# The fourth quarter of the summed shares: turned by the DMA engines in place of TensorE

## The chip, the core and the metric

The kernel runs on one core of one Trainium2 chip. The time is the device time of one launch in microseconds. Its engines here are TensorE (matmuls, PE in the profile, its weight loads PEld), VectorE (DVE), ScalarE (ACT), GpSimd (POOL) and SyncE (SP), which only issues DMAs. Each engine works through its own queue in order. Tiles lie in SBUF, and matmuls write to PSUM.

## The reference

Two layers over 512 tokens of 1024 channels, each made of a SwiGLU, a mixer (attention and a short convolution) and a second SwiGLU:

```python
def swiglu(h, w_gate, w_up, w_down):
    return (jax.nn.silu(h @ w_gate) * (h @ w_up)) @ w_down

for l in range(DEPTH):
    x = x + 0.5 * swiglu(rms_norm(x, ffn1_norm[l]), ffn1_wg[l], ffn1_wu[l], ffn1_wd[l])
    h = rms_norm(x, mix_norm[l])
    z = h @ w_in[l]
    ...
    x = x + jnp.concatenate([attn_out, conv_out], axis=-1) @ w_out[l]
    x = x + 0.5 * swiglu(rms_norm(x, ffn2_norm[l]), ffn2_wg[l], ffn2_wu[l], ffn2_wd[l])
return rms_norm(x, final_norm)
```

The inner width is 2816. All is float32.

## The kernel before, in words

The residual `x` lies transposed in SBUF for the whole run: 1024 channels are eight chunks of 128 (`xs[0]` to `xs[7]`), channels on the partitions and 512 tokens along a row. Two neighbouring chunks share a tile, so there are four pair tiles `xpair`, which the trace prints with the name `x`.

A float32 matrix is multiplied in three products. Each operand is split into a high part (`wh`, `xh`, `ah`: a ScalarE copy, L228 or L470) and a low part (`wl`, `xl`, `al`: a VectorE subtraction), and high by high, high by low and low by high are summed in PSUM (L318, L319, L321). Weights come from HBM as units of 512 KB into tiles `raw`, of which there are eight; SP issues their loads (L210) and `need_split` makes the high and low parts, two groups ahead of the matmuls. There are three `wh` and three `wl`.

A SwiGLU is a list of stages. An inner one (three of the four; the last one of the kernel ends in another way) runs `INNER`: blocks "p" and "w" of gate and up products, two stages "s" and a closing stage ("d", (9, 10)). A stage "s" multiplies by a part of `w_down` with seven products in place of eight. Its products have the tokens on the partitions, so their sum cannot be added to `x` as it is. The class `Apart` keeps this sum as tiles `apart`, one for each of four token tiles and two halves of the channels. It is treated in four quarters (o, t): half o of the channels and half t of the tokens. Quarter (0, 1) is the last to be complete, with the last product of the second stage "s".

A quarter comes back to `x` in one of two ways:

- by DMA: `Apart.send` lays the 16-bit halves of each float32 apart (ScalarE, L141, two copies of 128x1024 16-bit words) and SP issues two transposing DMAs (L909) into a tile `turned`. `Apart.back` joins the halves again (ScalarE, L922, two copies) and adds the result to `x` (VectorE, L926, two additions of 128x512).
- by TensorE: if a quarter was not sent, `Apart.back` makes eight 128x128 transposes with the identity into PSUM (L932) and adds from there (VectorE, L937, two additions).

Before the change, quarters (0, 0), (1, 1) and (1, 0) are sent at steps 3, 4 and 5 of the second stage "s" (`SENT_AT`), and (0, 1) is turned by TensorE.

The closing stage runs `down` over chunks in the order 4, 5, 6, 7, 0, 1, 2, 3. Each chunk takes 12 matmuls into an accumulator; VectorE adds half of it to the chunk of `x` (L1266). `BACK_AT` says behind which chunk a quarter is added back. Then `after(k)` prepares chunk k for the next stage's norm (class `into`): `norm.take` makes the gained high part on ScalarE (L470) and the low part on VectorE (L471), `norm.square` makes the squares on ScalarE (L476, L479, tile `nsq`) and sums them on VectorE (L480, tile `nacc`). `FINAL_AT` lets chunks 4 and 5 wait until behind chunk 5.

The next stage starts with groups of 24 matmuls over all eight chunks, again in the order 4 to 7, 0 to 3 for the first group. The sum of squares is split as well (`sqh` on ScalarE, `sql` on VectorE, L228), and two matmuls with ones (L535, tile `ssq`) stand behind the second chunk of the second group.

The loads of the weights of the next stage are held back (`state["hold"]`) through the last stage "s" and freed in the closing stage at chunk 5. `state["behind"]` then puts them in SP's queue behind the instruction `apart.last`, the last transposing DMA that was issued; at chunk 0 that is lifted.

ScalarE's and VectorE's queues are not written out by hand at this place: a scheduler orders the instructions when the program is built, within what the code ties down with `issue_after`.

Of the kernel before, what the change touches and what calls it, by code (L numbers as in the profile page):

```python
# [49 lines left out]


SENT_AT = {3: (0, 0), 4: (1, 1), 5: (1, 0)}
BACK_AT = {4: ((0, 1),), 5: ((1, 0),)}
FINAL_AT = {4: (), 5: (4, 5)}
STREAM_BACK_AT = {9: 0, 11: 1, 16: 2, 18: 3}
SCORES_AT = (5, 6, 7, 8, 9, 10, 12, 13)
# [19 lines left out]
def trunk_kernel(  # L76
# [35 lines left out]
    def g2(name, dt=F32, shape=(P, S)):  # L112
        return work.tile(list(shape), dt, tag="g2", bufs=14, name=name)
# [63 lines left out]
    def turn_rows(i):  # L177
        n = rows[i].shape[0]
        rp = psum("aux", [P, n], f"par_ps{i}")
        nc.tensor.transpose(rp, rows[i], ident[:n, :n])  # L180
        nc.scalar.copy(par[:, 16 * i : 16 * i + n], rp)
# [163 lines left out]
    def halves_of(n, wide, last):  # L345

        blocks = list(range(0, n, wide))
        return blocks[len(blocks) // 2 :] + blocks[: len(blocks) // 2] if last else blocks

    def down(rhs, fresh=False, last=False):  # L350

        wide = abreast(len(rhs))
        for c in halves_of(KC, wide, last):
            n, hi, lo = take_split()
            if fresh and c == 0:
                yield from enumerate(level(n, hi, lo, rhs, wide))
                continue
            for j in range(wide):
                cols = slice(j * P, (j + 1) * P)
                own = (f"{n}_{j}", hi[:, :, cols], lo[:, :, cols])  # L360
                tag = ("sc", "sc", "aux", "aux")[j] if fresh else "mm"
                yield c + j, group(rhs, own=own, tag=tag)
# [576 lines left out]
    def ahead(ops, at):  # L939
        return lambda step: ops.make(*at.get(step, ()))  # L940


    def ffn(norm, stages, after=None, late=None):
# [3 lines left out]
        def plain(b):  # L947
            gates = []

            def gate(acc):  # L950
                t = g2(f"gate_{norm.i}_{b}_{len(gates)}")
                nc.vector.tensor_mul(t, acc, norm.inv)
                nc.scalar.activation(t, t, AF.Silu)
                nc.vector.tensor_mul(t, t, norm.inv)
                gates.append(t)

            hi, lo = parts_of(f"a_{norm.i}_{b}")

            def up(j, acc):
                t = gates[j]  # L960
                nc.vector.tensor_mul(t, acc, t)
                split(hi[:, j, :], lo[:, j, :], t)

            if norm.i:
                accs = norm.groups(4)
                gate(accs[0])
                gate(accs[1])
                norm.scale()
                up(0, accs[2])
                norm.make("b11")  # L970
                up(1, accs[3])
            else:
                gate(opening[0])
                gate(opening[1])
                accs = norm.groups(4, opening)
                up(0, accs[2])
                up(1, accs[3])
                norm.scale((0,))
                norm.make("b11")
                norm.scale((1,))  # L980
            acts[b] = (hi, lo)
# [171 lines left out]
        def shared(b):  # L1153
            return Seven(lambda: [raws[b], raws[b + 2]], room_form, f"s_{norm.i}_{b}")

        def joined(between):


            def step(n):
                if n == 3:  # L1160
                    crossing[0].join_half(0)
                if n == 4:
                    crossing.pop(0).join_half(1)
                if crossing and isinstance(crossing[-1], Tail):
                    crossing[-1].during(n)
                between(n)

            return step
# [17 lines left out]
        def flush(n=1, *tag):  # L1186
            for _ in range(n):
                if pending:
                    pending.pop(0)(*tag)
# [3 lines left out]
        apart = Apart(f"{norm.i}")  # L1193
        for i, (what, b) in enumerate(stages):
            if what == "w" and stages[i + 1][0] == "s":
                ops = shared(sevens[0])
                winograd2(b, ahead(ops, {3: ("b11",), 4: ("b21",), 5: ("t2",), 6: ("t3",)}))
            elif what == "w":
                if after is None and b == 1:
                    end = apart = Finale()  # L1200
                between = late if b == 5 else end.step if end else None
                winograd2(b, between)
            if what == "s" and end:
                ends = [
                    Seven(full, None, f"e_{n}")
                    for n, full in enumerate((lambda b=b: [raws[b + 4], raws[b + 6]], raws[b + 8]))
                ]

                def between(step):
                    if 0 < step < 3:  # L1210
                        flush(2, "mm")
                    for at, n, operand in ((3, 0, "b11"), (4, 1, "b11"), (5, 0, "t2"), (6, 1, "t2")):
                        if step == at:
                            ends[n].make(operand)

                share(ops, 0.5, joined(between), apart, still=kept)
            elif what == "e":
                end.last(ends, kept)
                return
            elif what == "s" and b == sevens[0]:  # L1220
                then = shared(sevens[1])
                share(
                    ops,
                    0.5,
                    joined(ahead(then, {3: ("b11",), 4: ("b21",), 5: ("t2",), 6: ("t3",)})),
                    apart,
                    still=kept,
                )
            elif what == "s":

                def between(step):
                    if step == 1:
                        crossing[0].rejoin(1)
                    if step in (4, 5):
                        with tc.issue_after(state["rest"]):
                            crossing[0].parts(step - 4)
                    if step in SENT_AT:
                        apart.send(*SENT_AT[step])
                    if step == 0:
                        state["hold"] = closing[norm.i // 3 * 2 + norm.i % 3 // 2]  # L1240
                    if step == 6:
                        apart.back(0, 0)
                        apart.back(1, 1)

                share(then, 0.5, between, apart, behind=(1, 2, 3), on=kept)
            if what == "p":
                plain(b)
                if late:
                    turn_rows(1)
            if what != "d":  # L1250
                continue
            rhs = [(acts[k][0][:, j, :], acts[k][1][:, j, :]) for k in b if k in acts for j in range(2)]
            final = i + 1 == len(stages)
            if final:
                after.norm.order = halves_of(KC, 1, True)
            for c, acc in down(rhs, b == (0,), final):
                if b == (0,):
                    made = {0: "b21", 2: "t2", 5: "t3"}
                    if c in made:
                        norm.make(made[c])  # L1260
                if b == (0,) and norm.i == 0:
                    part = g2(f"down_{c}")
                    nc.scalar.activation(part, acc, AF.Copy, scale=0.5)
                    nc.gpsimd.dma_start(out=xs[c], in_=part, accum_op=ALU.add)
                else:
                    nc.vector.scalar_tensor_tensor(  # L1266
                        xs[c], acc, 0.5, xs[c], op0=ALU.mult, op1=ALU.add
                    )
                flush()
                if final:  # L1270
                    if c == 5:
                        state["hold"], state["behind"] = None, apart.last
                    if c == 0:
                        state["behind"] = None
                    for quarter in BACK_AT.get(c, ()):
                        apart.back(*quarter)
                    for k in FINAL_AT.get(c, (c,)):
                        after(k)

# [459 lines left out]
    for l in range(DEPTH):  # L1739
        n1, n2, n3 = Norm(3 * l + 1), Norm(3 * l + 2), Norm(3 * l + 3)  # L1740
        ffn(norm, INNER, into(n1), None if l else bias_steps())
        mix(l, n1, into(n2))
        if l + 1 < DEPTH:
            ffn(n2, INNER, into(n3))
        else:
            ffn(n2, LAST)
        norm = n3
# [30 lines left out]
```

## Time and profile before

| | |
|---|---|
| median of 3 runs | 1627.56 us (1626.3 to 1628.44) |
| the profiled execution's own time | 1627.75 us |
| its span, first to last instruction | 1626.0 us |
| mean granted TensorE clock | 0.998 |
| HBM read | 264.29 MB |

How to read the lines that follow: a row of the order in time has its start and its length in microseconds, the engine, the line of the kernel, the operation, the tile written and the tiles read, and how many alike were merged; in square brackets is the idle time of the engine just before, and what ended it. The length of a merged row runs from the first start to the last end. Instructions of one engine overlap a little, so what an instruction costs its queue is the distance from its start to that of the next. A row of a group has the count and the smallest, median and largest length in nanoseconds. A row of the waits names who waited for whom, the microseconds in total, how often, and the longest.

### The profile page before, as it was taken

To read this page: it belongs to the slowest core of one execution; us is meant where nothing else is said; L and a number is where in the kernel's file an instruction comes from. 1 tells how busy PE (TensorE), PEld (TensorE's weight loads), DVE (VectorE), ACT (ScalarE), POOL (GpSimd) and SP (SyncE) were. 2 spreads that over 40 slices of the span, in tenths; PEclk is the share of its full clock that TensorE was granted. 3 is DMA by queue.
4 is the path that set the end of the run, shared out by engine and by line. 5 is a ranking of instruction groups with operands and counts; after the bars stand their busy time and mean duration, and the time that the engine had idled before them with its cause. 6 is when DMAs were issued, how large, how long until landed. Compare 5 with 4: busy or idle time off the path is not lost.

```text
span 1626.0 us, 21171 instructions
## 1 busy us (share of the span) xinstructions
PE 1616.4 (99%) x7570; PEld 1350.2 (83%) x7570; DVE 1367.4 (84%) x1779; ACT 1177.3 (72%) x1510; POOL 223.6 (14%) x199
## 2 busy tenths in 40 slices
PE   9999999999999999999999999999999999999998
PEld 6888888888898888888888888888888988888887
DVE  6978797987899877797999777989788998677998
ACT  6767778867766577778865777788586767878665
POOL 1211111001121111111011111110012111111121
PEclk9999999999999999999999999999999999999999
DMA  8898989922597698999967999999136978999992
GB/s 264 203 246 208 221 200 241 238 71 78 131 233 181 170 226 212 216 212 240 235 147 187 215 216 225 204 244 228 48 91 157 231 151 211 225 226 226 245 248 75
DMA packets 307166, 318.12 MB, mean 196 GB/s; under 512 B 125612, under 2 KB 188660, under 8 KB 307060
## 3 DMA queue, kind: packets, MB, share of 16 engines
q1 hardware_dynamic: 265140, 230.76, 49.9%
q0 software_dynamic: 41200, 85.47, 30.6%
q8 instruction: 59, 0.97, 0.2%
q10 hardware_dynamic: 720, 0.53, 0.1%
q14 instruction: 47, 0.39, 0.1%
HBM read 264.29 MB, written 2.10 MB: 164 GB/s over the span
## 4 chain that ended last, share of the span: by engine, by line
PE 97%; DVE 1%; DMA 1%; ACT 0%; issue 0%; ACTq 0%; DVEq 0%
PE x L835 27%; PE y L835 13%; PE x_s L835 9%; PE acc L318 7%; PE acc L319 7%; PE acc L321 7%; PE w L835 7%; PE y_s L835 4%; PE x_m L820 3%; PE w_s L835 3%; PE y_m L820 1%; PE y_e L835 1%; PE acc L698 1%; PE x_e L835 1%; PE w_m L820 1%; DMA raw<-in_ffn_wd_dram 1%
## 5 line engine op out<-in xcount | busy, mean ns | idle before, releaser
L228 DVE TENSOR_TENSOR wl<-raw,wh 128x1024 fp32r<-128x1024 f32 (+1 forms) x493 | 598.8, 1222 | 172.1 <-ACT wh L228 171.5
L228 ACT CAST wh<-raw 128x1024 fp32r<-128x1024 f32 (+1 forms) x493 | 513.6, 1045 | 305.9 <-PE x L835 93.2
L318 PE MATMUL acc<-xh,wh 128*128 128x512 f32 x392 | 153.4, 393 | 0.5 <-ACT wh L228 0.5
L319 PE MATMUL acc<-xl,wh 128*128 128x512 f32 x392 | 153.3, 391 | 0.0
L321 PE MATMUL acc<-xh,wl 128*128 128x512 f32 x384 | 149.7, 390 | 0.0
L223 POOL DMA_DIRECT2D raw<-in_ffn_wu_dram x40 | 50.2, 1259 | 383.4 <-DMA raw<-in_ffn_wu_dram 247.5
L318 PEld LDWEIGHTS acc<-xh,wh 128*128 128x128 f32 x392 | 73.8, 188 | 15.1 <-ACT wh L228 0.6
L319 PEld LDWEIGHTS acc<-xl,wh 128*128 128x128 f32 x392 | 73.7, 188 | 14.5
L321 PEld LDWEIGHTS acc<-xh,wl 128*128 128x128 f32 x384 | 72.1, 188 | 15.1
L223 POOL DMA_DIRECT2D raw<-in_ffn_wg_dram x40 | 49.3, 1247 | 200.2 <-DMA raw<-in_ffn_wu_dram 93.7
L223 POOL DMA_DIRECT2D raw<-in_ffn_wd_dram x34 | 41.2, 1223 | 249.5 <-DMA raw<-in_ffn_wd_dram 60.6
L269 DVE TENSOR_TENSOR raw<-raw,raw 128x1024 f32<-128x1024 f32 x58 | 70.5, 1220 | 5.0 <-DMA raw<-in_ffn_wu_dram 3.5
L1099 ACT COPY raw_a<-turned 128x1024 uint16<-128x1024 uint16 x48 | 63.5, 1355 | 0.0
L835 PE MATMUL x<-wl,ft1h 128*128 128x512 f32 x160 | 62.4, 390 | 0.0
L835 PE MATMUL w<-wh,fb21h 128*128 128x512 f32 x160 | 62.4, 390 | 0.0
L835 PE MATMUL y<-wh,ft3h 128*128 128x512 f32 x160 | 62.4, 390 | 0.0
L835 PE MATMUL w<-wl,fb21h 128*128 128x512 f32 x160 | 62.4, 390 | 0.0
L835 PE MATMUL x<-wh,ft2l 128*128 128x512 f32 x160 | 62.3, 389 | 0.0
L835 PE MATMUL x<-wh,ft1l 128*128 128x512 f32 x160 | 62.3, 389 | 0.0
L835 PE MATMUL w<-wh,fb21l 128*128 128x512 f32 x160 | 62.3, 389 | 0.0
L835 PE MATMUL x<-wh,ft1h 128*128 128x512 f32 x160 | 62.3, 389 | 0.0
L835 PE MATMUL x<-wh,ft2h 128*128 128x512 f32 x160 | 62.3, 389 | 0.0
(517 smaller groups left out, 4545.6 us busy)
## 6 DMA issues: line engine op xcount, KB each, us to landing
raw<-in_ffn_wu_dram SPq DMA_DIRECT2D x127, 512.0 KB, 5.4
raw<-in_ffn_wd_dram SPq DMA_DIRECT2D x105, 512.0 KB, 6.0
raw<-in_ffn_wg_dram SPq DMA_DIRECT2D x86, 512.0 KB, 5.3
raw<-in_ffn_wu_dram POOLq DMA_DIRECT2D x40, 512.0 KB, 9.1
raw<-in_ffn_wg_dram POOLq DMA_DIRECT2D x40, 512.0 KB, 6.7
raw<-in_w_in_dram SPq DMA_DIRECT2D x36, 512.0 KB, 4.1
raw<-in_ffn_wd_dram POOLq DMA_DIRECT2D x34, 512.0 KB, 9.4
raw<-raw POOLq DMA_DIRECT2D x21, 512.0 KB, 8.2
```

What stands on the lines that cost most here:

```text
L223: nc.gpsimd.dma_start(out=r, in_=rows_of(*more), accum_op=ALU.add)
L228: return nc.scalar.copy(hi, raw), eng.tensor_sub(lo, raw, f32(hi))
L269: nc.vector.tensor_add(a11, a11, s1)
L318: nc.tensor.matmul(acc, hi[:, k, :], rhs[k][0], start=k == first, stop=False)
L319: nc.tensor.matmul(acc, hi[:, k, :], rhs[k][1], start=False, stop=False)
L321: nc.tensor.matmul(acc, lo[:, k, :], rhs[k][0], start=False, stop=k == last)
L698: nc.tensor.matmul(opening[n], (lo if part == "w" else hi)[:, k, :], xl if part == "x" else xh, start=n not in begun, stop=k == KC - 1 and ...
L820: nc.tensor.matmul(accs[c // 2][:, c % 2, :], w[:, k, cols], x_[:, 2 * h + k, :], start=start and c % 2 == 0 and h + k + i == 0, stop=h + ...
L835: nc.tensor.matmul(accs[u], x_[:, 2 * h + k, tok], w[:, k, :], start=start and h + k + i == 0, stop=h + k == 2 and i == 2, skip_group_chec ...
L1099: nc.scalar.copy(words(raws[self.b][:, c, :]), self.to[:, :, c, :])
```

## The change

The fourth quarter, (0, 1), is sent by DMA too. `send(0, 1)` stands in the closing stage behind chunk 5, behind the return of quarter (1, 0) and ahead of the line that frees the next weights; these are put behind the new transposing DMAs, as `apart.last` now names the last of them. The quarter is added to `x` behind chunk 0 in place of chunk 4. As it was sent, `back` takes the joins on ScalarE in place of the transposes on TensorE.

```diff
 SENT_AT = {3: (0, 0), 4: (1, 1), 5: (1, 0)}
-BACK_AT = {4: ((0, 1),), 5: ((1, 0),)}
+BACK_AT = {5: ((1, 0),), 0: ((0, 1),)}
 FINAL_AT = {4: (), 5: (4, 5)}
...
                 flush()
                 if final:
+                    for quarter in BACK_AT.get(c, ()):
+                        apart.back(*quarter)
                     if c == 5:
+                        apart.send(0, 1)
                         state["hold"], state["behind"] = None, apart.last
                     if c == 0:
                         state["behind"] = None
-                    for quarter in BACK_AT.get(c, ()):
-                        apart.back(*quarter)
                     for k in FINAL_AT.get(c, (c,)):
                         after(k)
```

## The prediction, made before the changed kernel ran

> **What bounds the kernel now.** I read the page first, then the view of waits for TensorE alone, then the order in time around the place that changes. The page gives the engines:
>
> ```profile
> PE 1616.4 (99%) x7570; PEld 1350.2 (83%) x7570; DVE 1367.4 (84%) x1779; ACT 1177.3 (72%) x1510; POOL 223.6 (14%) x199
> ```
>
> TensorE is busy for 99% of the 1626.0 us span. A busy share alone could hide waits between pipelined matmuls, so I asked for TensorE's waits over the whole execution. This is the complete answer:
>
> ```profile
> PE idle L151 <- DVE warm L645: 1.2, 1, 1.2
> PE acc L698 <- ACT xh L470: 0.8, 1, 0.8
> PE xt L664 <- DMA xin<-in_x_dram: 0.6, 1, 0.6
> PE acc L318 <- ACT wh L228: 0.5, 1, 0.5
> ```
>
> Four waits, 3.1 us, all at the opening. So every microsecond taken off TensorE's queue is worth a microsecond, if its operands still come in time, and every new wait of TensorE costs its full length. The question is therefore how close the operands are. The change acts at three places (the last stage of the three inner SwiGLUs, near 316, 796 and 1119 us). The first is worked out here. The view of busy time in stretches, with TensorE, weight loads, VectorE, ScalarE and GpSimd after the length:
>
> ```profile
> 313.30:324.20 10.90, 10.90 (x54) 9.12 (x53) 10.10 (x16) 9.40 (x10) 0.00 (x0) 1.00 1.05 303
> 324.20:335.90 11.70, 11.70 (x53) 9.69 (x52) 11.70 (x18) 8.14 (x14) 0.00 (x0) 1.00 0.58 167
> ```
>
> In the second stretch VectorE is busy 11.70 of 11.70 us. It has no room to catch up in. How near it is to TensorE shows in VectorE's last operations of the stage and in TensorE's use of them (order in time; start, length, engine, line):
>
> ```profile
> 319.97 1.28 DVE L937 TENSOR_TENSOR x<-x,back 128x512 f32<-128x512 f32 x2
> ...
> 321.76 1.28 DVE L926 TENSOR_TENSOR x<-x,back 128x512 f32<-128x512 f32 x2
> ...
> 328.49 1.22 DVE L228 TENSOR_TENSOR wl<-raw,wh 128x1024 fp32r<-128x1024 f32 x1
> 329.62 0.75 DVE L471 SCALAR_TENSOR_TENSOR xl<-x,par,xh 128x512 fp32r<-128x512 f32 x1
> 330.29 0.69 DVE L480 TENSOR_TENSOR nacc<-nacc,nsq 128x512 f32<-128x512 f32 x1
> 330.89 1.28 DVE L1266 SCALAR_TENSOR_TENSOR x<-acc,x 128x512 f32<-128x512 f32 x2
> ...
> 340.04 0.68 DVE L480 TENSOR_TENSOR nacc<-nacc,nsq 128x512 f32<-128x512 f32 x1
> 341.41 0.69 DVE L228 TENSOR_TENSOR sql<-nacc,sqh 128x512 fp32r<-128x512 f32 x1 [0.69 <-ACT sqh L228]
> ```
>
> ```profile
> 340.90 0.39 PE L319 MATMUL acc<-xl,wh 128*128 128x512 f32 x1
> 342.94 0.39 PE L535 MATMUL ssq<-sql,ones_r 128*128 128x512 f32 x1
> ```
>
> The last low part `xl` is done when the next operation starts, near 340.1, and TensorE uses it at 340.90: under 0.8 us to spare. The low part of the squares, `sql`, ends at 341.41 + 0.69 = 342.10 and is used at 342.94: 0.84 us to spare. The other two places have the same distance, 0.83 and 0.84 us:
>
> ```profile
> 821.94 0.69 DVE L228 TENSOR_TENSOR sql<-nacc,sqh 128x512 fp32r<-128x512 f32 x1 [0.69 <-ACT sqh L228]
> ...
> 1144.30 0.69 DVE L228 TENSOR_TENSOR sql<-nacc,sqh 128x512 fp32r<-128x512 f32 x1 [0.69 <-ACT sqh L228]
> ```
>
> ```profile
> 823.46 0.39 PE L535 MATMUL ssq<-sql,ones_r 128*128 128x512 f32 x1
> ...
> 1145.83 0.39 PE L535 MATMUL ssq<-sql,ones_r 128*128 128x512 f32 x1
> ```
>
> So one place stands for three.
>
> **What is removed: eight transposes on TensorE per place.** The group by line, then TensorE's order in time:
>
> ```profile
> L932 PE MATMUL back<-ident,apart x24: 270/272/273, 316.0 to 1119.6; 128*128 128x128 f32 x24
> ```
>
> ```profile
> 315.75 0.39 PE L321 MATMUL acc<-ah,wl 128*128 128x512 f32 x1
> 315.98 1.03 PE L932 MATMUL back<-ident,apart 128*128 128x128 f32 x8
> 316.77 0.48 PE L318 MATMUL acc<-ah,wh 128*128 128x512 f32 x1
> 317.09 0.40 PE L319 MATMUL acc<-al,wh 128*128 128x512 f32 x1
> ```
>
> One transpose lasts 0.272 us, but eight in a pipeline occupy 315.98 to 316.77, 0.79 us. A matmul of 512 columns starts every 0.227 us here (315.75 to 315.98), so without the transposes the one at 317.09 would start at 315.98 + 0.227 = 316.21. I take 0.88 us per place, 2.65 us for three. That is the most the change can win: 0.16% of the time.
>
> The Trainium skill ("TensorE: Matmul & The Clock Gate", Part 4: PE-mode transpose) gives about 275 ns for a 128x128 transpose inside a kernel. The row's 272 ns agrees as a length, but the starts 0.1 us apart decide here; by the page's figure taken as cost, 24 of them would be worth an estimated 6.6 us.
>
> The two additions on VectorE that read the turned quarter from PSUM (L937, 1.28 us the pair) become two that read it from SBUF (L926, 1.28 us the pair). I take zero for this, and the rows leave no other bound.
>
> **What is added on ScalarE and SP.** In the changed program's order ScalarE gets two lay-apart copies (L141) behind the joins of quarter (1, 0), and later two joins (L922) of quarter (0, 1): one between the first cast of the next weights and the gain step of chunk 7, one behind that gain step. SP gets two transposing DMAs in front of all the next weights. GpSimd's queue is not touched (0.00 us busy in the stretches above). ScalarE's order in time before, and its joins by line:
>
> ```profile
> 309.44 1.99 ACT L141 COPY halves<-apart 128x1024 uint16<-128x1024 uint16 x2
> ...
> 318.07 2.61 ACT L922 COPY back<-turned 128x1024 uint16<-128x1024 uint16 x2
> 320.50 1.08 ACT L228 CAST wh<-raw 128x1024 fp32r<-128x1024 f32 x1
> 323.08 0.73 ACT L470 ACTIVATE xh<-x,par 128x512 fp32r<-128x512 f32 x1 [1.50 <-DVE x L926]
> ...
> 326.64 1.03 ACT L228 CAST wh<-raw 128x1024 fp32r<-128x1024 f32 x1
> ...
> 329.24 0.62 ACT L479 ACTIVATE nsq<-x 128x512 f32<-128x512 f32 x1
> ...
> 340.76 0.62 ACT L228 CAST sqh<-nacc 128x512 fp32r<-128x512 f32 x1 [1.54 <-DVE nacc L480]
> ```
>
> ```profile
> L922 ACT COPY back<-turned x18: 1347/1362/1389, 312.3 to 1122.2; 128x1024 uint16<-128x1024 uint16 x18
> ```
>
> The lay-apart copies start at 320.50, where the cast stood; two last 1.99 us, one alone about 1.04, so the halves are ready at 321.54 and 322.49. They fall mostly into the 1.50 us that ScalarE sat idle: the cast then runs 322.40 to 323.35, and the six gain and square operations that ran from 323.08 to 326.64 (3.56 us) end at 326.91 instead. That alone is 0.27 us late, and harmless.
>
> Now the next weights. Before, they were issued at once behind the third quarter (SP's order in time, then the DMA issues of short windows: the first weight at 313.2, at 1116.4, the two at 794.3, and the transposing DMA before 313):
>
> ```profile
> 311.83 1.26 SPq L909 DMA_TRANSPOSE turned<-halves  x1
> 313.19 30.84 SPq L210 DMA_DIRECT2D raw<-in_w_in_dram  x12
> ```
>
> ```profile
> raw<-in_w_in_dram SPq DMA_DIRECT2D x1, 512.0 KB, 4.2
> ...
> raw<-in_w_in_dram SPq DMA_DIRECT2D x1, 512.0 KB, 3.8
> ...
> raw<-in_ffn_wg_dram SPq DMA_DIRECT2D x2, 512.0 KB, 5.1
> ...
> turned<-halves SPq DMA_TRANSPOSE x2, 2.7
> ```
>
> The first weight lay in SBUF at 313.19 + 4.2 = 317.4, and its cast came at 326.64: 9 us of cover. After the change SP waits for the halves: transposes at 321.54 and 322.85, the first weight 1.36 us later (311.83 to 313.19) at 324.2, landing at 328.4 (at 328.0 with 3.8 us, 329.3 with 5.1). ScalarE is ready for its cast at 326.91. So the cover is gone and ScalarE, whose queue is in order, waits 1.5 us. I take 4.2 us because at that place the load stands behind two transposes in the same way. The transposes land at 322.85 + 2.7 = 325.6 and hold nobody up.
>
> The Trainium skill ("DMA: Bandwidth & Descriptors", Anatomy of one DMA) fits a GpSimd-issued DMA as 2.0 us plus its bytes over 436 GB/s; an estimate for 512 KB is 3.2 us, and the three rows here are longer. By it the sum below would be 1.1 us instead of 4.1; the rows decide.
>
> Behind the waiting cast stand both joins, and behind these VectorE. Call the cast's start T. ScalarE: cast 0.95, join 1.25, gain step `xh` over at T + 2.93; its square 0.62 and the second join 1.36 over at T + 4.8. VectorE (steps by start to start: `wl` 1.13, `xl` 0.67, `nacc` 0.60, an addition 0.60): `xl` and `nacc` of chunk 7 to T + 4.24, the addition of chunk 0 to 4.84, the two additions of the quarter to 6.04, `wl` 7.17, `xl` and `nacc` of chunk 0 to 8.44, three additions 10.24, three pairs of `xl` and `nacc` 14.05, one `wl`, which the new order has in front, 15.18, and `sql` 15.87. With 0.05 us to TensorE that is T + 15.92 = 344.32, against 342.94 before: 1.38 us late, though TensorE itself would have come 0.88 us early. ScalarE's `sqh` is done by T + 14.8 and doesn't bind. On the way the `xl` of chunks 1 to 3 (T + 11.0, 12.2, 13.5) stop TensorE three times, within the same 2.26 us.
>
> Nothing makes the 1.38 us up again, since TensorE had no wait to give back behind this point. Three places: 4.1 us. The profiled execution took 1627.75 us (span 1626.0 and 1.75 around it) and becomes 1631.9; it lies 0.2 above the median of 1627.56, so the median becomes 1631.7. Bounds: T = 328.0 gives 0.98 a place (2.9 in all, 1630.5), T = 329.3 gives 2.28 (6.8, 1634.4). Later weights need no more: SP sends them right behind the first, and a group of 24 matmuls, 24 x 0.227 = 5.4 us, uses one.
>
> **The rivals.**
> *The weights come in time.* If ScalarE never waits, T = 326.91, `sql` reaches TensorE at 342.83, 0.11 us earlier a place: 1627.2. For it: 2 us of join work hide in ScalarE's idle time, as the 1.54 us before `sqh` suggest. Against it: the load would have to land within 2.7 us of its issue, and the fastest row is 3.8.
> *The transposes are won whole, so it isn't slower.* If VectorE's waits don't bind, because its additions at the place shift into gaps that I do not see, TensorE runs 2.65 us shorter: 1624.9. It decides at the last `xl`: done before 340.0 or not. Against it speaks the full second stretch. Should TensorE pay each transpose's length, 24 x 0.272 = 6.5 us: 1621.0; the 0.79 us for eight speaks against that.
> *The weights come later still.* If the load meets its own transposes in the DMA engines and takes 2 us longer than at 313, T = 330.4: 3.4 us a place, 1637.7. The spread of 3.8 to 5.1 allows a part of it.
>
> **How the numbers follow.** Forecast 0.56 (own range 1630.5 to 1634.4), weights in time 0.17, transposes won at their pitch 0.10, at their length 0.05, weights later still 0.12. I count as no change what lies within 0.2%, 3.3 us, about what a measurement of this kernel can tell: under 1624.3 is faster, over 1630.8 slower. Slower: most of the forecast (0.49) and the last rival (0.12), 0.61. Faster: 0.05 and a third of the 0.10, 0.08. The rest, 0.31, is no change. The range takes the forecast, the weights in time and over half of the last rival: 1626 to 1637.
>
> **What would show it.** ScalarE's first cast of the next weights idle about 1.5 us for the DMA of `raw`, at all three places; that DMA issued some 11 us later than before; TensorE waiting at L319 for `xl` and at L535 for `sql`, about 2.3 us a place, where before it waited for nothing; the transposes of L932 gone. If ScalarE's cast does not wait and TensorE still does, VectorE's order alone is the cause. If TensorE shows no waits there, the forecast is wrong and the time falls by 2.7 us.

## The result and the profile after

| | before | after |
|---|---|---|
| median | 1627.45 us (8 runs, 1625.95 to 1628.44) | 1631.80 us (8 runs, 1630.15 to 1634.69) |
| the profiled execution's own time | 1627.75 us | 1632.54 us |
| its span | 1626.0 us | 1630.8 us |

The ratio of after to before is 1.0026, with a 95% interval of 1.0017 to 1.0035. The changed kernel is slower by 4.35 us in the medians, where 1631.7 us was forecast.

The page of the changed kernel, engines first (busy time, share of the span, instructions):

```profile
PE 1618.0 (99%) x7546; PEld 1347.0 (83%) x7546; DVE 1367.8 (84%) x1779; ACT 1189.9 (73%) x1522; POOL 223.5 (14%) x199
```

TensorE has the 24 transposes less (7570 to 7546) and is shown busy for 1.6 us more with less work. The ends of its matmuls are modelled, so its busy time does not say where the 4.35 us went. The view of TensorE's waits, over the whole execution, names a wait that was not there before:

```profile
PE acc L319 <- DVE xl L471: 3.6, 9, 0.6
...
PE acc L318 <- ACT xh L470: 0.3, 1, 0.3
```

Nine waits for the low part `xl`: three at each of the three places. From there I go back along the chain: SP's order at the first place, then ScalarE's.

```profile
305.39 18.51 SPq L909 DMA_TRANSPOSE turned<-halves  x6
323.95 21.89 SPq L210 DMA_DIRECT2D raw<-in_w_in_dram  x12
```

```profile
325.97 0.63 ACT L479 ACTIVATE nsq<-x 128x512 f32<-128x512 f32 x1
328.51 1.05 ACT L228 CAST wh<-raw 128x1024 fp32r<-128x1024 f32 x1 [1.91 <-DMA raw<-in_w_in_dram]
329.47 1.36 ACT L922 COPY back<-turned 128x1024 uint16<-128x1024 uint16 x1
330.69 0.71 ACT L470 ACTIVATE xh<-x,par 128x512 fp32r<-128x512 f32 x1
...
331.83 1.34 ACT L922 COPY back<-turned 128x1024 uint16<-128x1024 uint16 x1
```

The loads are issued at 323.95, where they were at 313.19 before. ScalarE stands idle for 1.91 us for the first of them, and behind that cast come, in its order, a join, chunk 7's gain step and square, and the second join. VectorE's order shows what follows from it:

```profile
329.60 1.22 DVE L228 TENSOR_TENSOR wl<-raw,wh 128x1024 fp32r<-128x1024 f32 x1 [1.37 <-ACT wh L228]
331.44 0.75 DVE L471 SCALAR_TENSOR_TENSOR xl<-x,par,xh 128x512 fp32r<-128x512 f32 x1 [0.62 <-ACT xh L470]
...
333.31 1.28 DVE L926 TENSOR_TENSOR x<-x,back 128x512 f32<-128x512 f32 x2
...
341.24 0.74 DVE L471 SCALAR_TENSOR_TENSOR xl<-x,par,xh 128x512 fp32r<-128x512 f32 x1
...
342.50 1.21 DVE L228 TENSOR_TENSOR wl<-raw,wh 128x1024 fp32r<-128x1024 f32 x1
343.63 0.68 DVE L228 TENSOR_TENSOR sql<-nacc,sqh 128x512 fp32r<-128x512 f32 x1
```

It idles 1.37 and 0.62 us behind ScalarE, the quarter's two additions (1.20 us by their starts) come behind that, and its last low part of a chunk comes at 341.24 and `sql` at 343.63. TensorE at the same place, from the first matmul of the closing stage:

```profile
312.98 0.39 PE L318 MATMUL acc<-ah,wh 128*128 128x512 f32 x1
...
338.40 0.50 PE L318 MATMUL acc<-xh,wh 128*128 128x512 f32 x1
339.50 0.50 PE L319 MATMUL acc<-xl,wh 128*128 128x512 f32 x1 [0.60 <-DVE xl L471]
339.84 0.40 PE L321 MATMUL acc<-xh,wl 128*128 128x512 f32 x1
...
344.37 0.50 PE L535 MATMUL ssq<-sql,ones_r 128*128 128x512 f32 x1
```

**A measure for one place.** The time of a place on the clock shifts with the start of the execution (the first closing matmul of the first place lies between 310.8 and 313.3 us in the profiled executions of this study), a shift as large as the spread between runs. So I measure within a place: from the first closing matmul (312.98) to the matmul of `sql` (344.37) are 31.39 us. Before it is 29.68 us at each of the three places, from

```profile
313.26 0.39 PE L318 MATMUL acc<-ah,wh 128*128 128x512 f32 x1
```

and the `ssq` at 342.94 that the prediction shows. The other two places of the changed kernel, TensorE's start and end and ScalarE's waiting cast:

```profile
794.66 0.39 PE L318 MATMUL acc<-ah,wh 128*128 128x512 f32 x1
...
826.24 0.50 PE L535 MATMUL ssq<-sql,ones_r 128*128 128x512 f32 x1
...
1119.10 0.39 PE L318 MATMUL acc<-ah,wh 128*128 128x512 f32 x1
...
1150.11 0.51 PE L535 MATMUL ssq<-sql,ones_r 128*128 128x512 f32 x1
```

```profile
810.38 1.05 ACT L228 CAST wh<-raw 128x1024 fp32r<-128x1024 f32 x1 [1.96 <-DMA raw<-in_ffn_wg_dram]
...
1134.24 1.05 ACT L228 CAST wh<-raw 128x1024 fp32r<-128x1024 f32 x1 [1.54 <-DMA raw<-in_w_in_dram]
```

The places take 31.39, 31.58 and 31.01 us, 4.94 us more in all than before. The span grew by 4.8. So the whole loss lies in the three places. And in each of them the end follows from the waiting cast: it starts 15.53, 15.72 and 15.14 us behind the first matmul, and the matmul of `sql` starts 15.86, 15.86 and 15.87 us behind the cast.

### The profile page after: what moved, and what is told of

Same layout as the page of the kernel before. It is cut to its first block, busy times and chain, and to the rows that moved or that the text cites. A ratio compares the mean times of both kernels' runs of the same rounds, so it can differ in the third digit from the quotient of the medians.

```text
span 1630.8 us, 21140 instructions
## 1 busy us (share of the span) xinstructions
PE 1618.0 (99%) x7546; PEld 1347.0 (83%) x7546; DVE 1367.8 (84%) x1779; ACT 1189.9 (73%) x1522; POOL 223.5 (14%) x199
## 4 chain that ended last, share of the span: by engine, by line
PE 90%; ACT 2%; DVE 2%; DMA 2%; issue 2%; POOL 0%; SPq 0%; POOLq 0%; ACTq 0%; DVEq 0%
PE x L835 27%; PE y L835 13%; PE x_s L835 9%; PE w L835 7%; PE acc L319 6%; PE acc L318 6%; PE acc L321 6%; PE y_s L835 4%; PE w_s L835 3%; PE x_m L820 2%; PE y_m L820 1%; PE acc L698 1%; PE y_e L835 1%; PE x_e L835 1%; ACT xh L470 1%
## 5 line engine op out<-in xcount | busy, mean ns | idle before, releaser
L835 PE MATMUL x<-wl,ft2h 128*128 128x512 f32 x160 | 62.3, 389 | 0.0
L835 PE MATMUL y<-wh,ft3l 128*128 128x512 f32 x160 | 62.2, 389 | 0.0
```

The costliest lines, as they stand in the source:

```text
L835: nc.tensor.matmul(accs[u], x_[:, 2 * h + k, tok], w[:, k, :], start=start and h + k + i == 0, stop=h + k == 2 and i == 2, skip_group_chec ...
```

## The experiments

Theory: the loss is the joins' place in ScalarE's queue, behind a cast that waits for a load that is now late, with a VectorE that has no room to catch up. Rivals: the late loads by themselves, the joins by themselves, the transposes' worth being smaller or larger than taken, or VectorE's order ahead of the squares.

The return of the quarter is two things: the joins on ScalarE and the additions on VectorE (L926) that read what they write. In the runs that send the quarter and load late, both stand behind the waiting cast, or both ahead of it. What these runs show holds for the return as a whole; no run gives the price of the joins and of the additions apart.

"Place" below is the measure above. A second measure is used where an edit moves matmuls across `ssq`: from the first closing matmul to the first instruction behind the next stage's first groups (55.78 us before), summed over the three places, as the difference to the 167.35 us of before.

| run | places, us | three places to the end of the next groups, against before | ratio of times to before, 95% |
|---|---|---|---|
| before | 29.68, 29.68, 29.68 | 0 | |
| after | 31.39, 31.58, 31.01 | +5.32 | 1.0026 (1.0017 to 1.0035) |
| return left out | 28.79, 28.79, 28.78 | -2.68 | 0.9982 (0.9972 to 0.9993) |
| late loads only | 29.68, 29.71, 29.68 | +0.03 | 1.0003 (0.9992 to 1.0014) |
| weights first | 29.35, 29.43, 29.36 | -0.52 | 0.9992 (0.9982 to 1.0003) |
| weights first, low part later | 29.16, 29.23, 29.24 | -1.45 | 0.9987 (0.9978 to 0.9995) |
| joins behind chunk 7 | 29.93, 29.97, 29.98 | +0.83 | 1.0004 (0.9992 to 1.0015) |
| joins ahead of the late cast | 32.26, 32.26, 32.24 | +2.90 | 1.0014 (1.0005 to 1.0023) |
| the same, low parts later | 29.97, 29.88, 29.90 | +0.69 | 1.0002 (0.9993 to 1.0011) |
| after, low part later | 30.74, 31.35, 31.15 | +4.15 | 1.0015 (1.0006 to 1.0024) |
| after, loads later still | 33.94, 33.86, 35.25 | +8.26 | 1.0044 (1.0030 to 1.0058) |
| additions on GpSimd | 34.14, 33.96, 33.99 | +13.28 | 1.0081 (1.0068 to 1.0094) |
| the same, low part later | 32.33, 33.84, 34.49 | +11.68 | 1.0060 (1.0046 to 1.0073) |

In the row "joins ahead of the late cast" and in "after, loads later still" six or more further matmuls stand ahead of the matmul of `sql`, so the first column is long there for that alone, and only the second is to be compared.

**What the transposes are worth.** The return of quarter (0, 1) is left out.

```diff
-BACK_AT = {4: ((0, 1),), 5: ((1, 0),)}
+BACK_AT = {5: ((1, 0),)}
```

> The kernel before without the return of quarter (0, 1): the eight transposes on TensorE and the two additions on VectorE are left out at each of the three places, and nothing takes their place. Theory (a transpose costs TensorE its distance in the pipeline, 0.1 us): 2.65 us less than the kernel before, 1624.8 us, with no wait of TensorE at the places, as VectorE has 1.28 us less to do. Rival (each costs its length of 0.272 us): 6.5 us less, 1621 us. If VectorE were the limit even so: no change.

A place takes 28.79 us (310.80 to 339.59 at the first) in place of 29.68, and TensorE waits for nothing there in either run: eight transposes cost 0.89 us. Their length of 0.272 us each (2.18 us for eight) is not what they cost. The Trainium skill ("TensorE: Matmul & The Clock Gate", Part 4: PE-mode transpose) gives about 275 ns for one, which agrees with the length alone.

**Late loads alone.** The kernel before, with the next weights behind a small transfer that waits for the high part of chunk 4.

```diff
                     if c == 5:
-                        state["hold"], state["behind"] = None, apart.last
+                        state["behind"] = None
...
                         after(k)
+                        if k == 4:
+                            gate = small("gate", 1)
+                            state["behind"] = nc.sync.dma_start(
+                                gate, f32(after.norm.h[4][0][:, :1])
+                            ).ins
+                            state["hold"] = None
```

> The kernel before, transposes on TensorE kept, but SP's loads of the next weights stand behind a small DMA that reads the gained high part of chunk 4, so they are issued near 324 as in the changed kernel; ScalarE has no lay-apart copies and no joins more. Theory (late loads cost only together with the joins behind them): ScalarE's first cast waits about 1.9 us as in the changed kernel, but without joins and with VectorE's additions already done sql is ready at T + 14.1 = 342.7 and TensorE uses it at 342.94, so no loss: 1627.5 us, up to 1 us more. Rival (late loads alone carry the loss, by their wait or by traffic): 1631 to 1632 us.

SP's, ScalarE's and TensorE's order:

```profile
323.88 19.92 SPq L210 DMA_DIRECT2D raw<-in_w_in_dram  x12
```

```profile
327.84 1.06 ACT L228 CAST wh<-raw 128x1024 fp32r<-128x1024 f32 x1 [1.71 <-DMA raw<-in_w_in_dram]
```

```profile
312.67 0.39 PE L318 MATMUL acc<-ah,wh 128*128 128x512 f32 x1
...
342.35 0.39 PE L535 MATMUL ssq<-sql,ones_r 128*128 128x512 f32 x1
```

ScalarE waits for the load almost as long as in the changed kernel (1.71 against 1.91 us), and the place is 29.68 us, as before. Nothing of the quarter's return stands behind the cast here, neither joins on ScalarE nor additions on VectorE, which makes those from TensorE's transposes at 319.38, 8 us ahead of the cast. The scheduler also moved chunk 0's addition on VectorE ahead of the cast's `wl`. From the cast's own `wl` to `sql` VectorE takes 12.30 us at the first place (328.93 to 341.23) against 14.03 us in the changed kernel (329.60 to 343.63). Its list of operations between the two differs by three additions: the quarter's two (1.20 us) and chunk 0's (0.60 us). So additions on VectorE stand behind the wait as well as joins on ScalarE. Late loads without the return cost nothing.

**The return alone.** The changed kernel, but the next weights are freed at the start of the closing stage, so that five of them go out ahead of the two new transposes. The order on TensorE, VectorE and ScalarE is that of the changed kernel.

```diff
             if final:
                 after.norm.order = halves_of(KC, 1, True)
+                state["hold"], state["behind"] = None, apart.last
...
                     if c == 5:
+                        state["behind"] = None
                         apart.send(0, 1)
-                        state["hold"], state["behind"] = None, apart.last
```

> The changed kernel, but the next weights are freed at the start of the closing stage, so that SP sends five of them ahead of the two transposing DMAs; the queues of TensorE, VectorE and ScalarE hold the same work in the same order as in the changed kernel. Theory (the time is lost where ScalarE's first cast of the next weights waits for a load behind the transposes): that cast waits for no DMA, T is 1.5 to 1.9 us earlier at each place, sql reaches TensorE about 0.1 us earlier than in the kernel before, so about 1627.2 us, no more than 0.8 us from the kernel before; TensorE still waits about 0.75 us a place, since VectorE stays full. Rival (the two joins and VectorE's new order lose the time by themselves): 1631 to 1632 us as in the changed kernel. Third case (VectorE does not bind): the 2.65 us of the transposes are won, 1624.9 us.

```profile
313.19 5.83 SPq L210 DMA_DIRECT2D raw<-in_w_in_dram  x5
321.54 2.59 SPq L909 DMA_TRANSPOSE turned<-halves  x2
```

```profile
326.18 0.62 ACT L479 ACTIVATE nsq<-x 128x512 f32<-128x512 f32 x1
326.70 1.04 ACT L228 CAST wh<-raw 128x1024 fp32r<-128x1024 f32 x1
327.64 1.35 ACT L922 COPY back<-turned 128x1024 uint16<-128x1024 uint16 x1
```

```profile
313.19 0.39 PE L318 MATMUL acc<-ah,wh 128*128 128x512 f32 x1
...
342.54 0.50 PE L535 MATMUL ssq<-sql,ones_r 128*128 128x512 f32 x1
```

The cast follows the square without a gap, and 342.54 - 326.70 = 15.84 us later comes the matmul of `sql`: the same distance as in the changed kernel, from a cast that is 2 us earlier (13.51 us behind the first matmul, against 15.53). So the place follows the cast one for one over this whole stretch. It is 0.33 us shorter than before, so the return still costs 0.56 of the 0.89 us that the transposes gave.

Late loads alone cost nothing and the return alone doesn't make it slower; the two together cost 1.33 to 1.90 us a place. The wait was free where the work behind it had time to spare (late loads only) and moved the end by its length where it had none (2.02 us of cast, 2.04 us of place, between this run and the changed kernel).

**The return taken out from behind the cast.** The changed kernel, with loads as late, but the return behind chunk 7 and the casts of the next weights tied behind the joins.

```diff
-BACK_AT = {5: ((1, 0),), 0: ((0, 1),)}
+BACK_AT = {5: ((1, 0),), 7: ((0, 1),)}
...
-                state["cast"], state["rest"] = (i.ins for i in split(hi, lo, raw))
+                with tc.issue_after(state["join"]) if state["join"] else nullcontext():
+                    state["cast"], state["rest"] = (i.ins for i in split(hi, lo, raw))
...
-                        nc.scalar.copy(
+                        state["join"] = nc.scalar.copy(
...
-                        )
+                        ).ins
```

> The changed kernel with its late weights, but ScalarE's two joins of the last quarter and the steps of chunk 7 ahead of the first cast of the next weights, so that nothing that the squares need stands behind the cast that waits. Theory (the loss is the joins' place behind a waiting cast): although the loads are issued as late as in the changed kernel, a place is 29.7 to 30.3 us, against 31.3 in the changed kernel and 29.7 before; the time is 0 to 2 us over before. Rival (the late loads themselves, or the transposes' traffic, hold TensorE): a place stays at 31 us or more and the time about 5 us over before.

It lies between the two: 2.90 us over before by the second measure (2.3 by the times), where 0 to 2 and about 5 were expected. VectorE's order and TensorE's wait show why:

```profile
337.72 1.23 DVE L228 TENSOR_TENSOR wl<-raw,wh 128x1024 fp32r<-128x1024 f32 x1
338.85 0.76 DVE L472 SCALAR_TENSOR_TENSOR xl<-x,par,xh 128x512 fp32r<-128x512 f32 x1
...
342.54 1.23 DVE L228 TENSOR_TENSOR wl<-raw,wh 128x1024 fp32r<-128x1024 f32 x1 [1.06 <-ACT wh L228]
343.68 0.69 DVE L228 TENSOR_TENSOR sql<-nacc,sqh 128x512 fp32r<-128x512 f32 x1
```

```profile
339.66 0.50 PE L320 MATMUL acc<-xl,wh 128*128 128x512 f32 x1 [1.08 <-DVE xl L472]
```

The scheduler now put one `wl` (1.13 us) ahead of chunk 2's `xl` and another ahead of `sql`. So the run changed two things and did not tell the theories apart. The next one takes these low parts behind `sql`:

```diff
-            split(hi, lo, self.acc)
+            self.low = split(hi, lo, self.acc)[1].ins
...
-            accs = list(accs) or [group(self.h, order=self.order)]
+            late = self.order[0] == 4 and not accs
+            accs = list(accs) or [
+                group(self.h, own=take_split(1) if late else None, order=self.order)
+            ]
             parts = None if self.inv else self.parts()
+            if late:
+                with tc.issue_after(self.low):
+                    need_split(state["group"] - 1 + SPLIT_AHEAD)
```

> The run with the joins ahead of the late cast, with one difference: the low parts of the third and fourth next weights stand behind the low part of the squares on VectorE, so that neither is ahead of the low parts of chunks 2 and 3. The loads are as late as in the changed kernel. Theory (the loss is what stands behind the cast that waits): the wait of 1.08 us that the run before still had goes or falls under 0.5 us, and a place from its first closing matmul to the squares is 28.8 to 29.5 us, against 29.68 before and 31.3 in the changed kernel; the time 0.5 to 2.6 us under before. Rival (the late loads or the transposes' traffic hold TensorE by themselves): a place of 30 us or more, the time over that of before.

SP's order in that run, ScalarE's and TensorE's:

```profile
322.50 21.33 SPq L210 DMA_DIRECT2D raw<-in_w_in_dram  x12
```

```profile
325.04 2.58 ACT L929 COPY back<-turned 128x1024 uint16<-128x1024 uint16 x2
...
328.60 2.01 ACT L228 CAST wh<-raw 128x1024 fp32r<-128x1024 f32 x2
```

```profile
311.45 0.39 PE L319 MATMUL acc<-ah,wh 128*128 128x512 f32 x1
...
341.42 0.39 PE L542 MATMUL ssq<-sql,ones_r 128*128 128x512 f32 x1
```

The loads go out 322.50 - 311.45 = 11.05 us behind the first matmul, as late as in the changed kernel (10.97). The first cast starts 328.60 - 311.45 = 17.15 us behind the first matmul, 1.6 us later than in the changed kernel, and the place is 29.97 us, 1.42 us shorter. The 1.08 us wait is gone; two waits of up to 0.3 us for `xl` stay, so the place misses the expected 28.8 to 29.5 us by 0.4 us or more, and the time, expected 0.5 to 2.6 us under before, is that of before (a ratio of 1.0002). A place that is 1.42 us shorter with the loads as late and the same transposes still speaks against the rival that the late loads or the transposes' traffic stop TensorE.

Its counterpart is the changed kernel with the same edit of the low part, and nothing else:

> The changed kernel, loads and joins as it has them, with one difference: the low part of the third next weight stands behind that of the squares on VectorE. It is the counterpart of the run with the joins ahead of the late cast and the low parts behind the squares, and differs from it by the joins' place (and that of chunk 7's steps) alone. Theory (the joins behind the waiting cast make the low parts of chunks 1 to 3 late, and that alone costs most): the three waits for these low parts stay, and a place from its first closing matmul to the squares only falls from 31.3 to 31.0 to 31.2 us; the time is 4 to 4.7 us over before, and 3.4 us or more over that counterpart. Rival (VectorE's low part ahead of the squares is what costs): a place falls by its 1.13 us, to 30.2 us, and the time is about 1.6 us over before.

```profile
312.92 0.39 PE L318 MATMUL acc<-ah,wh 128*128 128x512 f32 x1
...
343.66 0.40 PE L541 MATMUL ssq<-sql,ones_r 128*128 128x512 f32 x1
```

```profile
327.96 1.05 ACT L228 CAST wh<-raw 128x1024 fp32r<-128x1024 f32 x1 [1.42 <-DMA raw<-in_w_in_dram]
```

`sql` reaches TensorE 343.66 - 327.96 = 15.70 us behind the cast, in place of 15.86: the low part ahead of the squares was worth 0.16 us, not its length, since the `xl` of chunks 1 to 3 are late already. The places, 30.74, 31.35 and 31.15 us, lie on both sides of the expected 31.0 to 31.2, as the cast starts 15.04, 15.65 and 15.44 us behind the first matmul. The two runs differ by the return's place: in the one before, the joins (with chunk 7's steps) stand ahead of the cast and the two additions at 326.71 and 327.65, ahead of the first next weight's `wl`; here they stand behind both, the additions from 332.77. The `wl` around them moved as well. The difference is 4.15 - 0.69 = 3.46 us over the three places. By the medians, each against its own before, it is 0.13% or 2.1 us; the profiled execution was the slowest of its eleven, and the time came out under the 4 to 4.7 us over before that were expected, at 2.4 us (1.0 to 3.9).

**VectorE's room, with the weights in time.** The edit of the low part on top of "weights first":

> The five next weights are issued ahead of the two new transposes (as in the run that sends the weights first), and the low part of the third next weight is formed behind the low part of the squares instead of ahead of it. Theory (with the weights in time, VectorE's sum of work up to the squares is what still holds TensorE): the step ahead of the squares is 1.13 us shorter, so the wait at the squares goes, while the one for the low part of chunk 3 (0.2 to 0.3 us) stays; a place from its first closing matmul to the squares falls from 29.4 to about 29.2 us, and the time to about 1.3 us under before. Rival (the rest of the transposes' worth is lost elsewhere, not on VectorE): the place stays at 29.35 to 29.43 us, the time 0.9 us under before.

29.16 to 29.24 us a place, as expected. It is the only version with the whole computation that is faster than before by more than the interval: 1625.28 us against 1626.90, a ratio of 0.9987. It keeps 1.45 of the transposes' 2.68 us.

**Joins later on ScalarE.** "Weights first", the joins behind chunk 7's square, and the low part later (the edit above):

```diff
-                    with tc.issue_after(state["cast"]):
+                    with tc.issue_after(behind or state["cast"]):
...
-                        apart.back(*quarter)
+                        apart.back(*quarter, after.norm.last if c == 0 else None)
```

> e1 (weights ahead of the transposes) with two changes of order: both joins of quarter (0, 1) stand behind chunk 7's gain step and square on ScalarE, and the low part of the third next weight stands behind sql on VectorE. Theory (VectorE's order decides what of the transposes is won): the last xl ends 0.1 us after TensorE would use it and sql on time, so about 0.7 us is won a place, 2.2 us in all, 1625.2 us. Rival (the order does not matter, VectorE's sum does): as e1, 1627.2 us.

A miss: the places grew to 29.93 to 29.98 us. VectorE's order there:

```profile
334.88 1.22 DVE L228 TENSOR_TENSOR wl<-raw,wh 128x1024 fp32r<-128x1024 f32 x1
336.02 1.28 DVE L1273 SCALAR_TENSOR_TENSOR x<-acc,x 128x512 f32<-128x512 f32 x2
337.49 0.75 DVE L471 SCALAR_TENSOR_TENSOR xl<-x,par,xh 128x512 fp32r<-128x512 f32 x1 [0.20 <-ACT xh L470]
```

With ScalarE's steps moved, the second weight's `wl` fell ahead of the additions of chunks 2 and 3, and the `xl` behind them came late. An edit that frees one queue moved the other.

**The additions on GpSimd.** "Weights first", and the two additions of quarter (0, 1) on the idle GpSimd.

```diff
-                    nc.vector.tensor_add(part, part, whole.rearrange("p (c s) -> p c s", c=2))
+                    eng = nc.gpsimd if (o, t) == (0, 1) else nc.vector
+                    eng.tensor_add(part, part, whole.rearrange("p (c s) -> p c s", c=2))
```

> The five next weights ahead of the transposes again, and the two additions of the quarter turned last made on GpSimd, which is idle there, instead of VectorE (1.28 us the pair less for VectorE). Theory (VectorE's sum binds once the weights are in time): TensorE waits for nothing at the three places, and a place falls from 29.4 to 28.8 us, the worth of the transposes: 2.65 us under before. Rival (GpSimd's additions, 1.4 to 1.6 us each by their rows elsewhere in this kernel, or their sharing of SBUF with VectorE, come too late for the gain step of chunk 0 or 1): a wait of TensorE for those chunks' high part appears, and the time is that of before or above.

GpSimd's order and ScalarE's:

```profile
329.32 3.52 POOL L927 TENSOR_TENSOR x<-x,back 128x512 f32<-128x512 f32 x2 [44.64 <-ACT back L922]
```

```profile
332.87 0.73 ACT L470 ACTIVATE xh<-x,par 128x512 fp32r<-128x512 f32 x1 [2.74 <-POOL x L927]
```

The rival holds, by more than its words: the pair takes 3.52 us on GpSimd where VectorE takes 1.28, chunk 0's gain step waits 2.74 us for it, and the time is 14 us over before. The Trainium skill ("GPSIMD Engine Reference", 4.1 Engine selection) has GpSimd about twice as slow as VectorE on additions of two tiles; here it is 2.75 times. An idle engine is no relief for a step that has only 0.8 us to spare. With the low part later as well:

> Both of the edits before together: weights ahead of the transposes, the two additions on GpSimd, the low part of the third next weight behind that of the squares. Theory: no more than the additions on GpSimd alone give, since TensorE can't run shorter than its own queue: a place at 28.8 us, 2.65 us under before, with more room ahead of the squares. Rival (VectorE still short of time by GpSimd's additions): this one is faster than the additions on GpSimd alone by 0.2 us a place or more.

11.68 us over before by the places: a little of it comes back, none of the gain.

**Loads later still.** The changed kernel, its loads behind a small transfer that waits for the high part of chunk 6.

```diff
-                        state["hold"], state["behind"] = None, apart.last
...
                         after(k)
+                        if k == 6:
+                            gate = small("gate", 1)
+                            state["behind"] = nc.sync.dma_start(
+                                gate, f32(after.norm.h[6][0][:, :1])
+                            ).ins
+                            state["hold"] = None
```

> The changed kernel with its next weights issued still later, behind a small transfer that waits for the high part of chunk 6, about 2.4 us after the changed kernel's. The rest is the changed kernel. Theory (whatever the first load is late, TensorE is late by the same): ScalarE's first cast of the next weights starts some 2.4 us later at each place, and a place grows by the same, from 31.3 to about 33.7 us; the time is 7 us over the changed kernel, 12 us over before. Rival (another step binds as well, so that a part of the lateness is covered, or the loads behind the first come late too): the place grows by clearly less, or by clearly more, than the cast's start.

```profile
330.60 1.05 ACT L228 CAST wh<-raw 128x1024 fp32r<-128x1024 f32 x1 [1.24 <-DMA raw<-in_w_in_dram]
```

The cast did start 2.2 us later, but the places grew by 8.26 - 5.32 = 2.94 us over the changed kernel's, not by 7. The scheduler had put chunk 7's gain step and square ahead of the cast, so less stood behind it. The run settles nothing on the slope. That comes from the runs that keep the changed kernel's order: its own three places and the three of "weights first", where the cast starts between 13.51 and 15.72 us behind the first matmul and `sql` follows 15.83 to 15.87 us behind it in all six.

## Why the prediction was right

- **The transposes, 0.88 us a place.** Measured 0.89, by leaving them out.
- **The issue of the first load, 324.2 against a first closing matmul at 313.26, so 10.94 us behind it.** Measured 323.95 - 312.98 = 10.97 us, and 11.11 and 10.97 at the other places. The halves and the transposes cost what their rows of before said.
- **The landing, 4.2 us.** This is the mis-sized term. By the DMA issues of the changed kernel the first load took 4.5, 4.5 and 4.1 us at the three places, and the cast started 4.56, 4.61 and 4.17 us behind its issue. ScalarE waited 1.91, 1.96 and 1.54 us, where 1.5 was forecast. The forecast cast start, T = 328.4, is 15.14 us behind the first matmul; measured 15.53, 15.72 and 15.14. The landing stayed within the bounds of 3.8 to 5.1 us that were kept for the range. The transposes ahead of the load explain little of it. From issue to cast are 3.96, 3.89 and 4.02 us without them (late loads only), and 4.07, 4.03 and 4.13 us with them in "after, low part later", about 0.1 us more. What made two of the changed kernel's loads some 0.5 us longer than these stays open.
- **The chain behind T, 15.92 us to the matmul of `sql`.** Measured 15.86, 15.86, 15.87. Each step of it stands in VectorE's order as forecast, with the three stops of TensorE for `xl` on the way. The forecast stop at L535 for `sql` is not in TensorE's list; the weight loads' list has it (last section), and the matmul starts 0.37 to 0.39 us behind the one before, where 0.23 us is the pitch. Against the run without the return TensorE lost 2.60, 2.79 and 2.23 us a place, where about 2.3 was forecast. A short wait for the high part `xh` of chunk 1 (0.3 us at the second place) was not foreseen; it lies within the same loss.
- **Nothing made up, three places alike.** Forecast 3 x 1.38 = 4.1 us; measured 1.71 + 1.90 + 1.33 = 4.94 us at the places and 4.35 us in the medians. The 0.8 us between 4.1 and 4.94 are the landing, 0.39 + 0.58 + 0.00, less 3 x 0.06 of the chain; the sum of that is 0.8. That the median came within 0.1 us of the forecast (1631.80 against 1631.7) is luck beyond this: the places of the profiled execution lost 0.8 us more than forecast, and the eight runs spread over 4.5 us.
- **The rivals.** "Weights in time" would have given 0.11 us a place under before; made so by hand, it gave 0.25 to 0.33. "The transposes are won whole" falls with the full VectorE: even with weights in time 0.56 of 0.89 us is eaten. "Later still" had T = 330.4; it was at most 0.6 us past the forecast.

What the prediction did not separate is that a late load and a late return are both needed. It priced them together, rightly, but a reader could have taken the late load for the cause; the run with late loads only shows that it isn't.

## What to carry to other kernels

When a step is moved behind a transfer, list what stands behind the waiting instruction in its engine's queue, and ask who has no room left: a wait of 1.6 to 1.7 us was free with time to spare behind it, and one of 1.5 to 2.0 us cost 1.3 to 1.9 us a place with the return behind it. Work taken off a bound engine is won only as far as the engine that gets it has room; here VectorE and ScalarE gave back 0.56 of 0.89 us even with the weights in time. A scheduler answers each edit by moving other instructions, so compare the order of all queues before reading an experiment: at least four runs here changed more than they were meant to.

## What the runs showed of the hardware

A wait of TensorE costs more than the list of waits says. In the changed kernel the matmul at 339.50 has 0.60 us of idle time by the list, but it starts 1.10 us behind the one before (338.40), where 0.23 us is the pitch, and the next starts 0.34 us later: 0.87 + 0.11 us are lost. The list is counted from a modelled end of the matmul before. Over the three places it shows 3.9 us, while TensorE lost 5.32 + 2.68 = 8.0 us against the run without the return. The same view for the weight loads (PEld) shows more of it, for the nine waits and for `sql` (five waits of 1.7 us in all, where before has two of 0.5 us):

```profile
PEld acc L319 <- DVE xl L471: 7.1, 9, 0.9
PEld ssq L535 <- DVE sql L228: 1.7, 5, 0.4
```

A loss is better taken from the starts of two matmuls than from the sum of waits.
